# Input stage of a hybrid attention block: gate products of 256 tokens, smaller norm groups, x scaled on GpSimd

## The chip, the core and the metric

The kernel runs on one NeuronCore of a Trainium2 chip (trn2). The metric is the device time of one execution in microseconds (us), the median of several executions. Engine names as in the profile: PE is TensorE's matrix unit and PEld its weight loads, DVE is VectorE, ACT is ScalarE, POOL is GpSimd, SP is SyncE, whose queue starts the DMA transfers here (SPq).

## What is computed

One encoder block on x of 2048 tokens by 1024 channels, float32. x is RMS-normed, one input projection gives the queries, keys and values of two attention mixers, two gate paths and merge logits; the mixers' outputs are gated, projected, merged, projected again and added to x. Only its beginning matters here:

```python
h = rms_norm(x, norm_gain[layer])      # x * rsqrt(mean(x*x) + eps) * gain
proj = h @ w_in[layer]
qa, ka, va, qb, kb, vb, ga, gb, mg = jnp.split(proj, split_idx, axis=-1)
...
ya = ya.reshape(bsz, S, A_WIDTH) * jax.nn.silu(ga)
yb = yb.reshape(bsz, S, B_WIDTH) * jax.nn.silu(gb)
```

## The kernel before, in words

**Precision.** Every float32 factor is split into a float16 high part and a float16 low part, and a product is three float16 products: high by high, high by low, low by high. XH and XL hold the two parts of the normed x, turned so that channels lie on the partitions: 8 chunks of 128 channels by 2048 tokens. gh and gl are the parts of one block of 128 gate columns, wh and wl those of one "unit" (the projections of one attention group).

**Input stage.** x comes in 16 tiles of 128 tokens (x0 to x15), one 512 KB transfer each, with 14 buffers. A tile passes these steps:
- ACT squares it and sums along the row (`x_square`, L444);
- for a group of tiles, DVE turns the sums into mean plus epsilon (`x_stats`, L448) and takes a first guess of the inverse root (L256); three Newton rounds follow (`rs_newton`), on DVE for a group of two (L270 to L272, 9 small operations) and on POOL for a group of four (L265 to L268, 12 small operations). The groups before are x0-1, x2-3, x4-7, x8-11, x12-15;
- DVE multiplies the tile by its inverse root (`x_scale`, L458);
- PE transposes it, in two halves h0 and h1 of four 128x128 blocks each, into one of three PSUM buffers `s` (`x_turn`, L464);
- for each half ACT copies the high part to XH (`x_hi`, L467) and DVE subtracts to get XL (`x_lo`, L471). Only then the PSUM buffer is free.

Beside it the weights of gate columns c = 0, 1 and 2 are prepared: gain on POOL (`g_gain`, L320, two halves), squares on ACT (L328), a sum over partitions by a tiny matrix product (L189), a power-of-two scale by some seven small DVE operations (L196 to L204, L341), high part on ACT (L346), low part on DVE (L350). The weights of the first unit take the same way: gain on POOL (L175, four parts), squares on ACT (L214), high part on ACT (L231), low part on DVE (L237). `head_gain` (L479 to L488, twice) and two small scalings are more small DVE work.

**Gate products.** For each quarter q of 512 tokens and for c = 0 and 1 PE makes 24 products of 128x512 (8 chunks, three products each, L304) into one PSUM bank; then come a tanh on ACT (L367), a multiplication on DVE (L374) and a store from SP. A quarter needs four x tiles. "Warm" products on a constant (L498) fill PE before that. Behind the stage comes the first unit's projection, whose products are those of L647.

**What sets the order.** All instructions are put into a heap by a planned time (`at`), and the times come from tables at the top of the file (X_SQ, X_CH, X_G, X_W and so on). `stream` issues the 24 products of a block spread over 5.2 planned us, and between them whatever is due. The planned times fix only the order on each engine; every engine then works through its own instructions strictly in that order, and waits where an operand is missing.

Of the kernel before, what the change touches and what calls it, by code (L numbers as in the profile page):

```python
# [21 lines left out]
F32 = mybir.dt.float32  # L22
# [3 lines left out]
OP = mybir.AluOpType  # L26
# [6 lines left out]
NT = S // 128  # L33
NCH = D // 128
# [45 lines left out]
N_PREP = (6.3, 7.15, 7.5)  # L80
B_GAP = (0.25, 0.2, 0.22)
Y_MAX = (0.02, 0.8, 0.84)
X_SQ = (5.098, 1.401, 9.779, 2.051)
X_CH = (9.3, 2.65, 1.024, 0.955, 1.155, 1.305)
X_ST = (1.3, 0.179)
X_G = (7.5, 15.282, 45.87)
X_GP = (2.1, 5.694, 7.094, 7.694, 8.894, 10.194)
X_W = (14.0, 38.0, 48.0, 1.1, 4.8, 5.2, 6.3, 0.6, 50.255)
X_WARM = (24, 16, 16, 16, 12)
X_TH = (0.8, 2.173, 3.5)  # L90
# [17 lines left out]
def block_kernel(tc, x, w_units, w_gate, w_mrg, w_brn, w_out, w_bra, gain, qkg, sink, bias_a, bias_b, b_merge, out):  # L108
    nc = tc.nc
    V = nc.vector  # L110
    A = nc.scalar
    G = nc.gpsimd
# [7 lines left out]
    sm = es.enter_context(tc.tile_pool(name="sm", bufs=4))  # L120
# [10 lines left out]
    done = set()  # L131
# [127 lines left out]
    def rs_newton(a, yv, r, n, pool):  # L259

        t = sm.tile([128, 10], F32, name="rs_t")
        tv = t[:, :n]
        for i in range(3):
            if pool:
                G.tensor_tensor(tv, yv, yv, OP.mult)  # L265
                G.tensor_tensor(tv, tv, a, OP.mult)  # L266
# [3 lines left out]
            V.tensor_tensor(tv, yv, yv, OP.mult)  # L270
            V.scalar_tensor_tensor(tv, tv, -0.5, a, OP.mult, OP.mult)
            V.scalar_tensor_tensor(r if i == 2 else yv, tv, 1.5, yv, OP.add, OP.mult)  # L272
# [21 lines left out]
        for f in tproj_list(ps, wh, wl, c0, q, nch, XHt, XLt, ch0):  # L294
            f()

    def tproj_list(ps, wh, wl, c0, q, nch=NCH, XHt=XH, XLt=XL, ch0=0):
        n = 3 * nch
        ts = slice(512 * q, 512 * q + 512)
        out = []  # L300
        for ch in range(ch0, ch0 + nch):
            for w, xx in ((wh, XHt), (wh, XLt), (wl, XHt)):
                i = len(out)
                out.append(lambda w=w, xx=xx, ch=ch, i=i: T.matmul(  # L304
                    ps[:], lhsT=w[:, ch, c0:c0 + 128], rhs=xx[:, ch, ts], start=(i == 0), stop=(i == n - 1)))
        return out


    gw = {}
# [8 lines left out]
    def g_gain(c, i):  # L318
        v = gw[c][0][:, 4 * i:4 * i + 4, :]
        G.tensor_tensor(v, v, gn[:, 4 * i:4 * i + 4].unsqueeze(2).to_broadcast([128, 4, 128]), OP.mult)  # L320

    def g_square(c):
        pool = gp if c > 1 else sp0
# [62 lines left out]
    def at(t, f, *args):  # L386
        seq[0] += 1
        heapq.heappush(heap, (t, seq[0], f, args))
# [8 lines left out]
    def chain(steps):  # L397

        steps = sorted(steps, key=lambda e: e[0])
        done = [0]  # L400

        def go(k):
            if done[0] < k or steps[k][1](*steps[k][2:]) is False:
                at(now[0] + .04, go, k)
            else:
                done[0] = k + 1

        for k, e in enumerate(steps):
            at(e[0], go, k)
# [10 lines left out]
    xts, xss, xps = {}, {}, {}  # L420
# [12 lines left out]
        V.tensor_scalar(bmh[:], bmt[:], 0.5, None, OP.mult)  # L433


    groups = {0: (0, 1), 1: (0, 1), 2: (2, 3), 3: (2, 3)}
    groups.update((t, tuple(range(t - t % 4, t - t % 4 + 4))) for t in range(4, NT))

    def x_square(t):
        g = groups[t]  # L440
        if t == g[0]:
            xss[g] = [sm.tile([128, 4], F32, name="xss")]
        jk = sp0.tile([128, D], F16, name="jk")
        A.activation(jk[:], xts[t][:], AF.Square, accum_out=xss[g][0][:, t - g[0]:t - g[0] + 1])  # L444

# [4 lines left out]

    def x_newton(g):
        ss, y = xss[g]
        xss[g] = sm.tile([128, 4], F32, name="xr")
        rs_newton(ss, y, xss[g][:, :len(g)], len(g), len(g) > 2)

    def x_scale(t):
        i = t - groups[t][0]
        V.tensor_scalar(xts[t][:], xts[t][:], xss[groups[t]][:, i:i + 1], None, OP.mult)  # L458

    def x_turn(t, h):  # L460
        xps[t, h] = ps = s_p.tile([128, 4, 128], F32, name="s")
# [36 lines left out]
            T.matmul(ps[:, 0:256], lhsT=v[:, 0:128], rhs=v, start=True, stop=True)  # L498


    for t in range(XT_BUFS):
        at(.01 * t, x_load, t)
    at(.015, lambda: nc.sync.dma_start(out=gn[:], in_=gain))
    at(.035, g_load, 0)
    at(.075, g_load, 1)
    at(2.0, small_loads)

    def scale_time(t):
        return X_CH[0] + X_CH[1] * t

    def ready_time(t):
        return scale_time(t) + sum(X_CH[2:])

    for t, n in enumerate(X_WARM):
        at(scale_time(t) + X_CH[2] - .05 if t < 4 else scale_time(3) + X_CH[2] + X_CH[5] + .05, warm, n)
    for t in range(NT):
        b = X_SQ[0] + X_SQ[1] * t if t < 4 else X_SQ[2] + X_SQ[3] * (t - 4)
        at(b, x_square, t)
        if t == groups[t][-1]:
            at(b + X_ST[0], x_stats, groups[t])  # L520
            at(b + X_ST[0] + X_ST[1], x_newton, groups[t])
        b = scale_time(t)
        at(b, x_scale, t)
        for h in range(2):
            b = scale_time(t) + X_CH[2] + X_CH[5] * h
            at(b, x_turn, t, h)
            at(b + X_CH[3], x_hi, t, h)
            at(b + X_CH[3] + X_CH[4], x_lo, t, h)
        if t < 2:
            for k in range(2):  # L530
                at(ready_time(t) + 1.0 + 1.2 * k, x_again, t, (XH, XL)[k])
        if t + XT_BUFS < NT:
            at(ready_time(t), x_load, t + XT_BUFS)
    for c in range(3):
        b = X_G[c]
        if c == 2:
            at(X_G[0] + X_GP[5] + .1, g_load, c)
        chain([(b + X_GP[0] * i, g_gain, c, i) for i in range(2)]
              + [(b + d, f, c) for d, f in zip(X_GP[1:], (g_square, g_sum, g_pow, g_hi, g_lo))])
# [16 lines left out]
    pos = 0  # L556
    for q in range(4):
        ready = ready_time(4 * q + 3) + .1
        pos = max(pos, ready)
        until(pos)  # L560
        assert all(("x", t, h) in done for t in range(4 * q, 4 * q + 4) for h in range(2))
        for c in range(2):
            mm, after = g_step(c, q)
            pos = stream(pos, 5.2, mm)
            for k, f in enumerate(after):
                at(pos + X_TH[k], f)
    until(1e9)
    st.close()
# [492 lines left out]
    for u in range(NU + 1):  # L1061
        t = 8 * u
# [33 lines left out]
    t = 0  # L1096
# [472 lines left out]
```

## Time and profile before

| | us |
|---|---|
| median of three runs | 1982.05 (1981.57 to 1983.27) |
| profiled execution, its own time | 1981.84 |
| span of that execution, first to last instruction | 1980.0 |
| PE busy | 1949.6 (98%) |
| DVE, ACT, POOL busy | 1310.7 (66%), 1029.3 (52%), 944.1 (48%) |
| first product of the first unit starts (end of the input stage on PE) | 80.57 |

"Span" runs from the first to the last instruction, and the execution's own time lies 1.84 us above it. In a row of the timeline stand the start in us, the length in us, the engine, the line, the operation with output and input, the count, and in brackets the idle time of the engine before it and who ended that. Matrix products overlap in the records (a 128x512 product lasts 0.38 us and the next one starts 0.22 us later), so the distance between starts is what one costs. Rows that stand for several equal instructions run from the first start to the last end.

### The profile page before, as it was taken

To read this page: it belongs to the slowest core of one execution; us is meant where nothing else is said; L and a number is where in the kernel's file an instruction comes from. 1 tells how busy PE (TensorE), PEld (TensorE's weight loads), DVE (VectorE), ACT (ScalarE), POOL (GpSimd) and SP (SyncE) were. 2 spreads that over 40 slices of the span, in tenths; PEclk is the share of its full clock that TensorE was granted. 3 is DMA by queue.
4 is the path that set the end of the run, shared out by engine and by line. 5 is a ranking of instruction groups with operands and counts; after the bars stand their busy time and mean duration, and the time that the engine had idled before them with its cause. 6 is when DMAs were issued, how large, how long until landed. Compare 5 with 4: busy or idle time off the path is not lost.

```text
span 1980.0 us, 47987 instructions
## 1 busy us (share of the span) xinstructions
PE 1949.6 (98%) x17654; PEld 1396.6 (71%) x17654; DVE 1310.7 (66%) x3485; ACT 1029.3 (52%) x2369; POOL 944.1 (48%) x2430
## 2 busy tenths in 40 slices
PE   8999999999999999999999999999999999999999
PEld 5567896678878898888988879898544444444444
DVE  6679877888768876667776778767733232876412
ACT  7467656776555566555666655656433343432200
POOL 4254556455547755547666676666410100232533
PEclk8999999999999999999999999999999999999999
DMA  6248986897849696667767776756732334778763
GB/s 248 80 90 163 180 164 140 145 191 149 177 87 197 116 181 122 130 137 164 148 135 143 146 162 128 138 122 126 171 104 93 119 110 169 221 232 271 250 240 143
DMA packets 589501, 308.47 MB, mean 156 GB/s; under 512 B 458064, under 2 KB 526800, under 8 KB 587984
## 3 DMA queue, kind: packets, MB, share of 16 engines
q1 hardware_dynamic: 589264, 305.39, 66.3%
q8 instruction: 138, 2.26, 0.5%
q14 instruction: 99, 0.81, 0.1%
HBM read 129.91 MB, written 65.27 MB: 99 GB/s over the span
## 4 chain that ended last, share of the span: by engine, by line
PE 52%; DVE 4%; POOL 3%; issue 2%; DMA 2%; ACT 1%; SPq 0%; DVEq 0%; POOLq 0%; ACTq 0%
PE pj L647 19%; PE fps L304 17%; PE fps L1446 7%; PE pj L304 5%; PE s L801 2%; PE pv L850 2%; POOL rs_t L265 1%; DVE rw L711 1%; POOL rs_t L266 1%; DMA kq<-spl 1%; DVE qss L699 0%; POOL rs_t L267 0%; POOL rw L718 0%; DMA yg<-ytd 0%; DVE pr L816 0%
## 5 line engine op out<-in xcount | busy, mean ns | idle before, releaser
L647 PE MATMUL pj<-wh,XH 128*128 128x128 f16 (+2 forms) x2816 | 708.5, 268 | 6.9 <-DVE vt L687 6.8
L647 PE MATMUL pj<-wl,XH 128*128 128x128 f16 (+2 forms) x2816 | 714.8, 268 | 0.0
L647 PE MATMUL pj<-wh,XL 128*128 128x128 f16 (+2 forms) x2816 | 712.7, 269 | 0.0
L647 PEld LDWEIGHTS <-XH 128*128 128x128 f16 x5632 | 579.1, 113 | 71.3 <-issue 9.2
L647 PEld LDWEIGHTS <-XL 128*128 128x128 f16 x2816 | 316.4, 112 | 25.9
L816 DVE CUSTOM_DVE_ANT_0 pr<-s,b,ubuf 128x256 f32<-128x256 f32 (+3 forms) x512 | 218.8, 464 | 41.2 <-PE s L801 38.8
L304 PEld LDWEIGHTS <-wh 128*128 128x128 f16 x1280 | 124.8, 98 | 150.3 <-issue 2.7
L265 POOL TENSOR_TENSOR rs_t<-rs_y 128x8 f32<-128x8 f32 (+2 forms) x345 | 110.8, 321 | 180.2 <-DVE rs_y L256 123.6
L833 DVE SCALAR_TENSOR_TENSOR p<-pr,p 128x512 f16<-128x512 f32 (+2 forms) x256 | 185.5, 724 | 16.8 <-ACT p L829 16.2
L711 DVE TENSOR_TENSOR rw<-rw,qr 128x512 f32<-128x512 f32 (+1 forms) x112 | 119.2, 1064 | 101.8 <-POOL qr L268 87.8
L718 POOL TENSOR_TENSOR rw<-rw,g 128x128 f32<-128x128 f32 (+1 forms) x224 | 135.5, 624 | 84.3 <-DVE rw L711 58.6
L175 POOL TENSOR_TENSOR wraw<-wraw,gn 128x768 f32<-128x768 f32 (+1 forms) x80 | 108.3, 1360 | 130.1 <-DMA wraw<-in_w_mrg_dram 130.1
L829 ACT ACTIVATE p<-pr 128x512 f16<-128x512 f32 (+2 forms) x256 | 158.9, 621 | 11.6 <-DMA pt<-p 5.6
L304 PE MATMUL fps<-Y,wh 128*128 128x512 f16 x512 | 152.3, 379 | 0.3 <-DVE kp L1382 0.2
L801 PE MATMUL s<-kq 128*128 128x128 f16 (+1 forms) x1856 | 147.8, 218 | 4.7 <-DMA kq<-spl 4.5
L801 PEld LDWEIGHTS <-kq 128*128 128x128 f16 x2016 | 130.0, 98 | 28.8 <-issue 5.4
L666 ACT ACTIVATE rw<-pj 128x256 f32<-128x256 f32 (+1 forms) x224 | 86.1, 384 | 122.7 <-PE pj L647 119.2
L733 POOL COPY spl<-spl 128x256 f16<-128x256 f16 (+1 forms) x224 | 93.9, 448 | 116.9 <-DVE spl L728 115.2
L304 PE MATMUL pj<-XH,gh 128*128 128x512 f16 x384 | 145.5, 379 | 0.0
L304 PE MATMUL pj<-XL,gh 128*128 128x512 f16 x384 | 145.5, 379 | 0.0
L304 PE MATMUL pj<-XH,gl 128*128 128x512 f16 x384 | 145.5, 379 | 0.0
L1446 PE MATMUL fps<-wt,M 128*128 128x512 f16 x672 | 145.2, 379 | 0.0
(196 smaller groups left out, 3549.7 us busy)
## 6 DMA issues: line engine op xcount, KB each, us to landing
wraw<-in_w_units_dram SPq DMA_DIRECT2D x56, 384.0 KB, 4.6
mtd<-mm SPq DMA_DIRECT2D x56, 256.0 KB, 3.8
M<-mtd SPq DMA_DIRECT2D x8, 1792.0 KB, 9.7
mgd<-fg SPq DMA_DIRECT2D x40, 256.0 KB, 2.1
zd<-z SPq DMA_DIRECT2D x128, 66.0 KB, 1.9
zz<-zd SPq DMA_DIRECT2D x64, 132.0 KB, 3.0
xt<-in_x_dram SPq DMA_DIRECT2D x16, 512.0 KB, 8.9
gtd<-yo SPq DMA_DIRECT2D x32, 256.0 KB, 2.9
```

The costliest lines, as they stand in the source:

```text
L175: G.tensor_tensor(v, v, gn[:, c0:c0 + 2].unsqueeze(2).to_broadcast([128, 2, n]), OP.mult)
L265: G.tensor_tensor(tv, yv, yv, OP.mult)
L304: out.append(lambda w=w, xx=xx, ch=ch, i=i: T.matmul(ps[:], lhsT=w[:, ch, c0:c0 + 128], rhs=xx[:, ch, ts], start=(i == 0), stop=(i == n - 1)))
L647: out.append(lambda lhs=lhs, rhs=rhs, ch=ch, a=a, b=b, k=k: T.matmul(ps[:, a:b], lhsT=lhs[:, ch, :], rhs=rhs[:, ch, a:b], start=(k == 0), ...
L711: V.tensor_tensor(q, q, self.rr[:, :n].unsqueeze(2).to_broadcast([128, n, HD]), OP.mult)
L718: G.tensor_tensor(q[:, i, :un.nq, :], q[:, i, :un.nq, :], g, OP.mult)
L733: G.tensor_copy(sp[:, i, nh:, :, :], sp[:, i, nq:nh, ::-1, :])
L801: T.matmul(self.sv[j][:, o:o + k1 - k0], lhsT=q[:, h, :], rhs=kt[:, un.nq + kh + v * un.nk, k0:k1], start=(v == 0), stop=(v == 1))
L816: V.tensor_tensor_reduce(out=self.pv[:, j, self.p0:self.p0 + W], in0=self.sv[j], in1=un.bias[:, self.h0 + j, self.b0:self.b0 + W], scale=I ...
L829: A.activation(self.sp[:, :128 * n], self.pr, AF.Copy, scale=PSC)
L833: V.scalar_tensor_tensor(self.sp[:, 128 * n:], self.pr, PSC, self.sp[:, :128 * n], OP.mult, OP.subtract)
L1446: mm.append(lambda ch=ch, k=k, w=w, i=i: T.matmul(ps[:], lhsT=m[:, a, ch, k, :], rhs=wt[w][:, b, ch, :], start=(i == 0), stop=(i == 11)))
```

## The change

- A gate block is now 24 products of 128x256 for 256 tokens, so it needs two x tiles. The order is (c, h), with h the eighth of the tokens: (0,0), (0,1), (1,0), (1,1), and then c = 0, 1 for each h from 2 to 7. Two blocks share a PSUM bank, and tanh, multiplication and store follow the second. The banks alternate between two pools.
- x is normed in the groups x0-1, x2-3, x4-5, x6-9, x10-13, x14-15. All but the first do their Newton rounds on POOL.
- `x_scale` runs on DVE for x0 and x1 and on POOL for the other 14 tiles.
- The gain of c = 1 moves from POOL to DVE. The weights of c = 0 are loaded right behind x1 and gn, and those of c = 1 behind x5.
- 46 warm products are left of 84. The copies of the first two tiles behind the last one (`x_again`) come later.
- All planned times of the stage are new.

```diff
-X_WARM = (24, 16, 16, 16, 12)
+X_SC = (9.2, 9.9, 15.8, 17.475, 23.6, 24.8, 33.0)
+X_WARM = (34, 6, 6, 0)
...
-    def tproj_list(ps, wh, wl, c0, q, nch=NCH, XHt=XH, XLt=XL, ch0=0):
+    def tproj_list(ps, wh, wl, c0, q, nch=NCH, XHt=XH, XLt=XL, ch0=0, n=512):
+        ts = slice(n * q, n * q + n)
...
-    groups = {0: (0, 1), 1: (0, 1), 2: (2, 3), 3: (2, 3)}
-    groups.update((t, tuple(range(t - t % 4, t - t % 4 + 4))) for t in range(4, NT))
+    groups = {t: g for g in ((0, 1), (2, 3), (4, 5), (6, 7, 8, 9), (10, 11, 12, 13), (14, 15)) for t in g}
...
-        rs_newton(ss, y, xss[g][:, :len(g)], len(g), len(g) > 2)
+        rs_newton(ss, y, xss[g][:, :len(g)], len(g), g[0] > 0)
...
-        V.tensor_scalar(xts[t][:], xts[t][:], xss[groups[t]][:, i:i + 1], None, OP.mult)
+        (V if t < 2 else G).tensor_scalar(xts[t][:], xts[t][:], xss[groups[t]][:, i:i + 1], None, OP.mult)
...
-    for q in range(4):
-        ready = ready_time(4 * q + 3) + .1
-        pos = max(pos, ready)
+    for c, h in [(0, 0), (0, 1), (1, 0), (1, 1)] + [(c, h) for h in range(2, 8) for c in range(2)]:
+        pos = max(pos, ready_time(2 * h + 1) + .1, (X_G0, X_G1)[c][5] + .1)
         until(pos)
...
+        if h % 2 == 0:
+            banks[c] = (pv_p if q % 2 else pj_p).tile([128, 512], F32, name="pv" if q % 2 else "pj")
+        ps = banks[c]
+        o = 256 * (h % 2)
+        pos = stream(pos, 2.6, tproj_list(ps[:, o:o + 256], gh, gl, 0, h, n=256))
+        if h % 2:
+            for k, f in enumerate(gate_steps(ps, c, q, ih, None)):
                 at(pos + X_TH[k], f)
```

**Place 1, tiles x6 and x7.** On PE before, from x4 on, the transposes of a half tile (L464, four of them) are set apart from the next ones by gate products (L304): by three between the halves of x4, shown here, and by six after that, x6 and x7 included:

```order
L464 MATMUL s<-idf,xt 128x128 x4
L304 LDWEIGHTS gh
L304 MATMUL pj<-XH,gh 128x512
L304 LDWEIGHTS gh
L304 MATMUL pj<-XL,gh 128x512
L304 LDWEIGHTS gl
L304 MATMUL pj<-XH,gl 128x512
L464 MATMUL s<-idf,xt 128x128 x4
```

Now all 16 transposes of x6 and x7 (both halves of both tiles, L467) stand together behind the 144th gate product, the last of block (1,2), and right behind them comes block (0,3), which reads x6 and x7:

```order
L308 LDWEIGHTS gl
L308 MATMUL pv<-XH,gl 128x256
L467 MATMUL s<-idf,xt 128x128 x16
L308 LDWEIGHTS gh
L308 MATMUL pv<-XH,gh 128x256
```

No gate product stands any more between these transposes and the first product that needs their result. On POOL, now, the last of the 12 Newton operations for x6-9 (output `xr`) is followed by the scaling of x6, the fourth part of the first unit's gain (`wraw`), and the scaling of x7 and x8:

```order
L272 TENSOR_TENSOR xr<-rs_t,rs_y 128x4
L461 TENSOR_SCALAR xt<-xt,xr 128x1024
L179 TENSOR_TENSOR wraw<-wraw,gn 128x768
L461 TENSOR_SCALAR xt<-xt,xr 128x1024 x2
L324 TENSOR_TENSOR graw<-graw,gn 128x512 x2
L461 TENSOR_SCALAR xt<-xt,xr 128x1024
```

Before, POOL scaled no x tile, and all four parts of the unit's gain came behind the last Newton round.

**Place 2, tiles x7 to x9 on ACT.** Before, the copies to XH (L467) of the later tiles come in runs of four with a tanh (L367) between, since all squares of x are done by then:

```order
L367 ACTIVATE yo<-pj,ubuf 128x512
L467 ACTIVATE XH<-s 128x4x128 x4
L367 ACTIVATE yo<-pj,ubuf 128x512
L467 ACTIVATE XH<-s 128x4x128 x4
L367 ACTIVATE yo<-pj,ubuf 128x512
L467 ACTIVATE XH<-s 128x4x128 x3
```

Now there stand, from the two copies of x7 on (first row): the squares of x13, a copy of x8, squares of the unit's weights (`wsq`), a copy of x8, the squares of x14 and of gate column 2, weights again, a copy of x9, a tanh, a copy of x9:

```order
L470 ACTIVATE XH<-s 128x4x128 x2
L447 ACTIVATE jk,xss<-xt 128x1024
L470 ACTIVATE XH<-s 128x4x128
L218 ACTIVATE wl,wsq<-wraw 128x768
L470 ACTIVATE XH<-s 128x4x128
L447 ACTIVATE jk,xss<-xt 128x1024
L332 ACTIVATE gh,gsq<-graw 128x1024
L218 ACTIVATE wl,wsq<-wraw 128x768
L470 ACTIVATE XH<-s 128x4x128
L371 ACTIVATE yo<-pv,ubuf 128x512
L470 ACTIVATE XH<-s 128x4x128
```

So weight and square work has moved between the copies. In the same way the squares of x9 now stand behind the copies of x5.

**Place 3, the last tiles on DVE.** Now, behind the second `head_gain` (its last two operations are the first rows), the low parts of the unit's weights (`wl`) and the multiplications for the gates (`yo`) stand between the subtractions (`XL`) of x14 and x15:

```order
L490 TENSOR_SCALAR ubuf<-ubuf 128x1
L491 TENSOR_SCALAR ubuf<-ubuf 128x1
L241 SCALAR_TENSOR_TENSOR wl<-wraw,ubuf,wh 128x768
L474 TENSOR_TENSOR XL<-s,XH 128x4x128
L436 TENSOR_SCALAR nsnk<-snk 128x8
L437 TENSOR_SCALAR bmh<-bmt 128x16
L378 SCALAR_TENSOR_TENSOR yo<-yo,pj 128x512
L241 SCALAR_TENSOR_TENSOR wl<-wraw,ubuf,wh 128x768
L474 TENSOR_TENSOR XL<-s,XH 128x4x128 x2
L378 SCALAR_TENSOR_TENSOR yo<-yo,pj 128x512
L474 TENSOR_TENSOR XL<-s,XH 128x4x128
```

Before, the last subtraction of the stage (first row) is followed by the scale of gate column 2, and only then by the first `wl` (L237):

```order
L471 TENSOR_TENSOR XL<-s,XH 128x4x128
L196 TENSOR_REDUCE wm_913<-pt 128x1
L197 TENSOR_SCALAR wm_913<-wm_913 128x1
L199 TENSOR_SCALAR pw_p<-wm_913 128x1
L200 TENSOR_SCALAR pw_p<-pw_p 128x1
L203 TENSOR_SCALAR ubuf<-pw_p 128x1
L204 RECIPROCAL ubuf<-ubuf 128x1
L341 TENSOR_SCALAR ubuf<-ubuf 128x1
L237 SCALAR_TENSOR_TENSOR wl<-wraw,ubuf,wh 128x768
```

What moved is the order of DVE alone: all four `wl`, and with them the low part of gate column 2, now come ahead of the last subtraction.

More of the change, by code (lines that the diff above doesn't have):

```diff
@@ L441, in x_square @@
         if t == g[0]:
-            xss[g] = [sm.tile([128, 4], F32, name="xss")]
+            xss[g] = [sm.tile([128, 5], F32, name="xss")]
         jk = sp0.tile([128, D], F16, name="jk")
@@ L498, in warm @@
             T.matmul(ps[:, 0:256], lhsT=v[:, 0:128], rhs=v, start=True, stop=True)
+    at(0, warm, X_WARM[0])
     for t in range(XT_BUFS):
@@ L554, in stream @@
         return pos + share
-    pos = 0
-    for q in range(4):
-        ready = ready_time(4 * q + 3) + .1
-        pos = max(pos, ready)
+    pos, banks = 0, {}
+    for c, h in [(0, 0), (0, 1), (1, 0), (1, 1)] + [(c, h) for h in range(2, 8) for c in range(2)]:
+        pos = max(pos, ready_time(2 * h + 1) + .1, (X_G0, X_G1)[c][5] + .1)
         until(pos)
[L561 to L565, printed above, removed]
+        assert ("g", c) in done and all(("x", t, k) in done for t in (2 * h, 2 * h + 1) for k in range(2))
+        gh, gl, ih = gw[c][:3]
+        q = h // 2
+        if h % 2 == 0:
[5 more added lines that the diff above has]
+            for k, f in enumerate(gate_steps(ps, c, q, ih, None)):
                 at(pos + X_TH[k], f)
```

47 lines of the change are left out of this document (24 added, 23 removed).

## The prediction

> **What bounds the kernel now.** I read the page's busy times first, then busy times by stretch, then the timeline.
>
> ```profile
> PE 1949.6 (98%) x17654; PEld 1396.6 (71%) x17654; DVE 1310.7 (66%) x3485; ACT 1029.3 (52%) x2369; POOL 944.1 (48%) x2430
> ```
>
> ```profile
> 0.00:28.04 28.04, 19.20 (x118) 14.54 (x118) 16.49 (x45) 19.45 (x34) 12.62 (x26) 0.82 0.94 357
> 28.04:80.57 52.53, 52.50 (x294) 30.56 (x295) 41.81 (x96) 34.49 (x59) 15.41 (x33) 1.00 0.17 67
> 80.57:130.00 49.43, 49.12 (x334) 29.27 (x333) 27.00 (x61) 21.70 (x48) 23.76 (x71) 1.00 0.37 101
> ```
>
> A stretch's row has its length, then the busy time of PE, PEld, DVE, ACT and POOL, the granted clock, the DMA share and GB/s. PE bounds the kernel: it has no gap from 28.04 to 80.57, where the first unit starts, and hardly one behind that (49.12 of 49.43 us). So whatever moves the end of the input stage moves the end of the kernel by as much. The change can only gain in the first 28 us, in which PE warms up or waits for x.
>
> PE's work, by the distance between starts:
>
> ```profile
> 28.54 0.38 PE L304 MATMUL pj<-XH,gh 128*128 128x512 f16 x1
> 28.75 0.38 PE L304 MATMUL pj<-XL,gh 128*128 128x512 f16 x1
> ...
> 50.11 0.60 PE L464 MATMUL s<-idf,xt 128*128 128x128 f32 x4
> 50.55 0.38 PE L304 MATMUL pj<-XH,gh 128*128 128x512 f16 x1
> ```
>
> ```profile
> 700.34 0.27 PE L647 MATMUL pj<-wh,XH 128*128 128x256 f16 x1
> ...
> 701.87 0.27 PE L647 MATMUL pj<-wh,XL 128*128 128x256 f16 x1
> ```
>
> A 512-wide product costs 0.215 us, four transposes 0.44. The two 256-wide products are 14 steps apart, 0.109 each, every one with its own weight load. So the halved products cost nothing much: 384 x 0.109 = 41.9 against 192 x 0.215 = 41.3. What counts is when PE starts and where it stops again.
>
> **The first product.** Tiles arrive one after another:
>
> ```profile
> 8.57 1.06 ACT L444 ACTIVATE jk<-xt 128x1024 f16<-128x1024 f32 x1 [1.70 <-DMA xt<-in_x_dram]
> ...
> 12.81 1.06 ACT L444 ACTIVATE jk<-xt 128x1024 f16<-128x1024 f32 x1 [1.84 <-DMA xt<-in_x_dram]
> ```
>
> Here ACT waited for x2 and for x4. x2 is the third 512 KB, x4 the sixth (gate column 0 lies between): 4.24 / 3 = 1.4 us each. Now column 0 comes third, so x2 arrives at 10.0 and x3 at 11.4. The groups up to 80.6 us, with the mean in ns behind the comma:
>
> ```profile
> L467 ACT ACTIVATE XH<-s 128x512 f16<-128x512 f32 x32 | 18.8, 593 | 13.8 <-PE s L464 13.5
> L444 ACT ACTIVATE jk<-xt 128x1024 f16<-128x1024 f32 x16 | 16.8, 1053 | 6.2 <-DMA xt<-in_x_dram 6.1
> L367 ACT ACTIVATE yo<-pj,ubuf 128x512 f32<-128x512 f32 x7 | 4.8, 684 | 1.1 <-PE pj L304 0.9
> L214 ACT ACTIVATE wl<-wraw 128x768 f16<-128x768 f32 x4 | 3.3, 836 | 0.0
> L328 ACT ACTIVATE gh<-graw 128x1024 f16<-128x1024 f32 x3 | 3.1, 1048 | 0.0
> L444 ACT ACTIVATION_READ_ACCUMULATOR jk<-xt 128x1 f32 x16 | 3.1, 192 | 0.0
> ```
>
> ```profile
> L471 DVE TENSOR_TENSOR XL<-s,XH 128x512 f16<-128x512 f32 x32 | 21.6, 687 | 8.2 <-ACT XH L467 8.1
> L374 DVE SCALAR_TENSOR_TENSOR yo<-yo,pj 128x512 f32<-128x512 f32 x7 | 4.8, 682 | 0.1
> L237 DVE SCALAR_TENSOR_TENSOR wl<-wraw,ubuf,wh 128x768 f16<-128x768 f32 x4 | 4.0, 1014 | 0.2 <-ACT wh L231 0.2
> L350 DVE SCALAR_TENSOR_TENSOR gl<-graw,ubuf,gh 128x1024 f16<-128x1024 f32 x3 | 3.8, 1278 | 0.0
> ```
>
> ```profile
> L175 POOL TENSOR_TENSOR wraw<-wraw,gn 128x768 f32<-128x768 f32 x4 | 6.6, 1688 | 0.0
> L320 POOL TENSOR_TENSOR graw<-graw,gn 128x512 f32<-128x512 f32 x6 | 6.3, 1062 | 9.8 <-DMA graw<-in_w_gate_dram 9.8
> L475 POOL COPY XH<-XH 128x1024 f16<-128x1024 f16 x2 | 2.1, 1034 | 3.1 <-ACT XH L467 3.1
> masks.py:199 POOL TENSOR_SCALAR_AFFINE_SELECT idf<-idf 128x128 f32<-128x128 f32 x1 | 0.3, 292 | 0.1
> ```
>
> From 10.0 ACT squares x2, column 0 and x3 in a row, 1.25 each (with 0.19 for the sum): 13.75. On PE the norm product of column 0 now stands ahead of the second half of x0, which waits for that square. Then the first XH (0.59), its XL (0.69), and, queued behind it on DVE, mean and guess of x2-3 (0.4): 15.45. Their Newton rounds move to POOL:
>
> ```profile
> 7.31 0.16 DVE L270 TENSOR_TENSOR rs_t<-rs_y 128x2 f32<-128x2 f32 x1
> ...
> 9.07 0.75 DVE L458 TENSOR_SCALAR xt<-xt,xr 128x1024 f32<-128x1024 f32 x1
> ...
> 22.26 1.28 DVE L350 SCALAR_TENSOR_TENSOR gl<-graw,ubuf,gh 128x1024 f16<-128x1024 f32 x1
> ...
> 22.48 1.12 POOL L266 TENSOR_TENSOR rs_t<-rs_t,xss 128x4 f32<-128x4 f32 x1
> ...
> 43.77 0.20 POOL L265 TENSOR_TENSOR rs_t<-rs_y 128x4 f32<-128x4 f32 x1 [5.61 <-DVE rs_y L256]
> ...
> 44.88 0.20 POOL L265 TENSOR_TENSOR rs_t<-rs_y 128x4 f32<-128x4 f32 x1
> ```
>
> Nine operations on DVE took 9.07 - 7.31 = 1.76; on POOL four take 1.11, so twelve 3.3. The pair in the middle shows a lock: a 0.20 us operation of POOL lasts 1.12 and ends with DVE's `gl`. The column-1 gains that move to DVE have no row there: between the XL row (0.69) and POOL's own (1.06); I take 0.69, and DVE has slack at that point. With one collision (0.7) POOL's rounds end at 19.4.
>
> **Scaling on POOL** has no row. The low end is DVE's own 0.75 (the 9.07 row), the high end twice POOL's 1.06 for 512 elements, 2.1. But those 512 are read from two tensors, and the scaling reads one; the one-input rows, 1024 in 1.03 and 128 float32 in 0.29, give about 0.8 ns an element for either type. I take 1.03. Of the Trainium skill, GPSIMD Engine Reference, section 8, calls DVE about twice as fast for elementwise work; that estimate, 2 x 0.75, would add some 1.4 us over the three scalings of the chain below. Its section 4.1 puts one-input operations near line rate, and the copy row agrees with that.
>
> So x2 is scaled at 20.4, turned at 21.4 (0.94 on a slow clock), and the first gate product starts there, 7 us earlier than before.
>
> **Block (0,0)** has 24 products, three half tiles and a norm product ahead of block (0,1): 2.6 + 1.3 + 0.3 = 4.2 at full clock. But PE has been idle for some 3 us before it, and then
>
> ```profile
> 24.20 0.94 PE L464 MATMUL s<-idf,xt 128*128 128x128 f32 x4 [1.08 <-DVE XL L471]
> ```
>
> ```profile
> 25.00:26.00 1.00, 1.00 (x6) 0.50 1.05 393
> 28.00:29.00 1.00, 0.93 (x7) 1.00 1.04 406
> ```
>
> the granted clock (behind the count) stays at half from 24.2 to 28: 3.8 us that do 1.9 of work. Block (0,1) starts at 21.4 + 4.2 + 1.9 = 27.5 (26.5 if tiles land earlier or the clock holds, 28.2 if column 1's seven small DVE operations delay the last XL).
>
> **Tiles x6 and x7.** From 27.5 PE has 120 products and four half tiles: 13.1 + 1.8, and would be through at 42.4. x9's square stands behind the copies of x5, whose last transposes come 53 products and four half tiles into this: 35.1. XH 0.6, square 1.25, mean and guess 0.4: 37.3. POOL: Newton 3.3, x6 1.03, a gain 1.69, x7 1.03: 44.4. Then transposes 0.44, two XH 1.18, XL 0.69: block (0,3) starts at **46.7**. Of the wait 1.8 us is transposing and **2.5 idle**.
>
> **ACT from x7 to x9.** Behind the last XH of x7 (46.0) come two squares of x (2.49), column 2's (1.24), two of the unit's weights (2.06), four XH (2.37) and a tanh (0.68): 8.84, then XL 0.69. Block (0,4) starts at **55.5**. PE's own work (48 products 5.25, four half tiles 1.75, a norm product 0.3) ends at 54.0: **1.5 idle**.
>
> **DVE to x15.** From 55.5 to the last XL its queue holds 12 XL (8.25), 4 `yo` (2.75), 4 `wl` (4.05), `gl` (1.28), two scales of 7 and 6 small operations at 1.76 / 9 = 0.196 (2.55), mean, guess and two small ones (0.75), and two `head_gain`:
>
> ```profile
> 64.10 0.22 DVE L479 SCALAR_TENSOR_TENSOR g<-qg 128x64 f32<-128x64 f32 x1
> ...
> 65.66 0.68 DVE L374 SCALAR_TENSOR_TENSOR yo<-yo,pj 128x512 f32<-128x512 f32 x1
> ```
>
> 1.56 each. Together 22.75. `gl` and `wl` then meet POOL's scalings of x13 to x15 in the lock: nothing if they miss each other, 2 us if each waits; I take 1. The last XL ends at **79.3**. PE alone (144 products 15.7, twelve half tiles 5.3, a norm product) would be there at 76.8: **2.5 idle**.
>
> **Sum.** The last two blocks take 5.25: 84.5 in place of 80.57, **+4.0 us**: the early start is given back in three waits. The profiled execution took 1981.84; with +4.0 that is 1985.9, and against the median 1982.05 1986.1. The removed warm products are waited for by nobody, and the later copies on POOL are read only by later units.
>
> **Rivals.** A difference under 0.2%, 4 us, cannot be told from none; my forecast lies on that border.
> - *The three waits as worked out*, 0.45: bounds of first block (-1.0, +0.7), lock (-1, +1) and gains give 1983.7 to 1988.5. 0.28 of it is slower.
> - *Part of the waits is absorbed*, since one that ends earlier shortens the next: first block at 26.5, no lock, x9's square up to a microsecond sooner: 0 to +2, 1982 to 1984. 0.16, same.
> - *The early start is kept*: if x7 is turned before PE is through with the 144th product, at 42.4, so POOL done with it 4.3 us sooner than worked out, and ACT and DVE keep ahead after that. PE's work behind 21.4 is 41.9 + 27 x 0.44 + 0.9 = 54.7: the end is 76.1, or 78.0 with the slow clock, 1976.5 to 1979.5. For it speaks that before PE ran 52 us without a gap with DVE at 80%; against it the orders, which leave no product between x7's transposes and their user. 0.16; 0.10 of it faster.
> - *Scaling costs 2.1*: x2, x6 and x7 lie on the chain, +3.2 more: 1989.3. Against it the copy row. 0.11, slower.
> - *The clock falls again in the waits*: a stall at half clock costs up to 1.9 us as above; behind x7 1.5 of it is hidden by ACT's queue, before the last blocks nothing: +2.3 more, 1988.4. 0.12, slower. The Trainium skill's TensorE: Matmul & The Clock Gate (Part 1) lets the clock fall only after an idle window of about 3.4 us; by that these waits would leave it alone, but the 24.20 row shows a fall after a wait of 1.08 in a thinly filled stretch.
>
> Faster 0.10, same 0.17 + 0.16 + 0.06 = 0.39, slower 0.51. The range runs from the rival that keeps the start to the dearer scaling, 1979.0 to 1990.0.
>
> **What would show it.** In the new profile: the first gate product near 21.4 at half clock; scaling on POOL near 1.03; PE idle for DVE's XL around 43 to 47, around 54, and before the last two blocks; the first unit at 84.5. It is wrong if PE has no gap behind block (0,0), if `gl` or the 256-wide products are what waits, or if the first unit starts at the old time and later work pays.

## The result, and the profile after

The changed kernel takes 1995.45 us in the median of four runs (1994.67 to 1998.08), and the kernel before, beside it, 1982.66. The ratio is 1.006, with a 95% interval from 1.0045 to 1.0074: slower, and above the upper end of my range, 1990.0. The profiled execution took 1995.38 us, 13.54 more than that of before.

The line of the page that answers to the first one shown of before, and two stretches of the input stage, in the same columns as before (length; busy time of PE, PEld, DVE, ACT and POOL; granted clock; DMA share; GB/s):

```profile
PE 1948.1 (98%) x17808; PEld 1413.3 (71%) x17808; DVE 1302.4 (65%) x3466; ACT 1029.4 (52%) x2369; POOL 980.6 (49%) x2466
```

```profile
28.00:40.00 12.00, 12.00 (x111) 10.87 (x110) 7.29 (x12) 9.84 (x18) 11.14 (x12) 1.00 0.41 159
40.00:95.00 55.00, 43.31 (x361) 37.43 (x360) 28.83 (x70) 28.97 (x52) 42.56 (x53) 0.94 0.06 25
```

The page's busy line hides the loss: PE is at 98% as before, and POOL at 49% after 48%. The stretch shows it. Before, PE had no gap from 28.04 to 80.57; now it is idle for 11.7 of the 55 us behind 40, DVE and ACT are only half busy, and POOL is the busiest of the three helpers. Whom PE waits for in the first 100 us (us in total, times, longest):

```profile
PE s L467 <- POOL xt L461: 17.2, 7, 5.9
PE s L467 <- DVE xt L461: 4.6, 1, 4.6
PE pv L501 <- DVE ones L142: 1.1, 1, 1.1
PE pv L308 <- DVE XL L474: 0.3, 1, 0.3
```

Seven waits are for a tile scaled by POOL. The waits that I had worked out for ACT's queue and for DVE's last subtractions are not there: ACT itself waits for PE's transposes (26.6 us in all between 20 and 95). On POOL, at the place of x6 to x8:

```profile
42.53 2.84 POOL L461 TENSOR_SCALAR xt<-xt,xr 128x1024 f32<-128x1024 f32 x1
45.34 1.47 POOL L179 TENSOR_TENSOR wraw<-wraw,gn 128x768 f32<-128x768 f32 x1
46.80 5.66 POOL L461 TENSOR_SCALAR xt<-xt,xr 128x1024 f32<-128x1024 f32 x2
```

One scaling takes **2.84 us**, where I took 1.03 and put the upper bound at 2.1. On PE the first, the second and the third wait, and the first product of the unit:

```profile
22.80 1.12 PE L467 MATMUL s<-idf,xt 128*128 128x128 f32 x4 [5.87 <-POOL xt L461]
...
45.43 1.09 PE L467 MATMUL s<-idf,xt 128*128 128x128 f32 x8 [1.31 <-POOL xt L461]
49.69 1.62 PE L467 MATMUL s<-idf,xt 128*128 128x128 f32 x8 [3.17 <-POOL xt L461]
...
95.19 0.33 PE L655 MATMUL pj<-wh,XH 128*128 128x384 f16 x1
```

The first unit starts at 95.19 in place of 80.57, **+14.6 us**, and 13.5 of it stand at the end. That is the theory tested below: the price of POOL's scaling made the loss, and POOL became the bound of the stage. The rivals: the order, with x6 and x7 turned in one bunch, costs the time whoever scales; or POOL's other new work (Newton rounds) does.

### The profile page after: what moved, and what is told of

The parts are those of the page before. It is cut to its first block, busy times and chain, and to the rows that moved or that the text cites. A ratio compares the mean times of both kernels' runs of the same rounds, so it can differ in the third digit from the quotient of the medians.

```text
span 1993.5 us, 48316 instructions
## 1 busy us (share of the span) xinstructions
PE 1948.1 (98%) x17808; PEld 1413.3 (71%) x17808; DVE 1302.4 (65%) x3466; ACT 1029.4 (52%) x2369; POOL 980.6 (49%) x2466
## 4 chain that ended last, share of the span: by engine, by line
PE 75%; POOL 9%; DVE 7%; issue 5%; DMA 3%; ACT 1%; SPq 1%; DVEq 0%; POOLq 0%; ACTq 0%
PE pj L655 30%; PE fps L308 19%; PE pj L308 11%; PE fps L1454 7%; PE s L809 4%; PE pv L858 3%; POOL rs_t L269 1%; POOL xt L461 1%; POOL rs_t L270 1%; DVE rw L719 1%; POOL rs_t L271 1%; DVE qss L707 1%; DVE pr L824 1%; DMA xt<-in_x_dram 1%; POOL rw L726 1%
## 5 line engine op out<-in xcount | busy, mean ns | idle before, releaser
L269 POOL TENSOR_TENSOR rs_t<-rs_y 128x8 f32<-128x8 f32 (+3 forms) x351 | 110.6, 315 | 172.8 <-DVE rs_y L260 122.3
L1397 POOL TENSOR_TENSOR kp<-kp,fg 128x512 f32<-128x512 f32 x32 | 44.5, 1392 | 209.8 <-DVE fg L1390 121.0
L308 PE MATMUL pj<-XH,gh 128*128 128x512 f16 (+1 forms) x384 | 139.4, 363 | 0.0
L732 ACT ACTIVATE spl<-rw 128x512 f16<-128x512 f32 (+1 forms) x112 | 72.1, 643 | 130.4 <-POOL vt L682 84.8
```

The costliest lines, as they stand in the source:

```text
L308: out.append(lambda w=w, xx=xx, ch=ch, i=i: T.matmul(ps[:], lhsT=w[:, ch, c0:c0 + 128], rhs=xx[:, ch, ts], start=(i == 0), stop=(i == n - 1)))
```

## The experiments

In all of them "the first unit" is the start of the first product of that kind in the profiled execution, 80.57 before and 95.19 after. The execution's own time less that start lies between 1899.0 and 1903.8 us in all kernels of the study that were profiled for their time, so the start tells what the stage costs to about 2 us, in that execution. The profiled execution lies between 2.6 us below and 4.4 us above the median of its kernel, so a start and a ratio need not agree to better than that. Ratios are to runs of the kernel before on the same chip.

### All scaling on DVE

```
-        (V if t < 2 else G).tensor_scalar(xts[t][:], ...
+        V.tensor_scalar(xts[t][:], ...
```

> The change with one part of it undone: all sixteen tiles are scaled on DVE. The price theory (a scaling takes 2.84 us on POOL, and nothing else of the change costs more than I worked out): no wait for POOL's xt is left on PE, and the first unit product starts between 81 and 85 us instead of 95.2, so that the run takes 1982 to 1987 us. The order theory (the bunched transposes and their queues cost the time whoever scales): PE still waits over 10 us between 28 and 80 us, the first unit product starts at 90 or later, 1990 us or more. What is left over 1982 is the price of all the rest of the change; my prediction worked out +4.0 for it.

Measured: the first unit at 82.00, ratio 0.999 (0.9981 to 0.9998), 13.2 us of the 14.6 gone. PE still waits for scaled tiles, now DVE's:

```profile
PE s L467 <- DVE xt L461: 10.7, 6, 4.9
```

4.9 of this is the wait for x0 and 3.1 that for x2, ahead of the first gate product, which leaves 2.7 for four others. The rest of the change, all but the engine of the scaling, is worth +1.4 us on the stage, where I had worked out +4.0.

### The kernel before, with its scaling on POOL

```
-        V.tensor_scalar(xts[t][:], ...
+        (V if t < 2 else G).tensor_scalar(xts[t][:], ...
```

> The kernel before with that part alone: tiles x2 to x15 are scaled on POOL. The price theory: 2.84 us each, four in a row for a group of four, 11.4 us where DVE took 3.0; POOL also has the Newton rounds and gains, and PE eats a group of four in 13.8 us, so that POOL becomes the bound: the first unit product moves from 80.6 to between 89 and 95 us, 1990 to 1997 us. The rival, that the groups and the order of the changed kernel are needed to make a loss: scaling stays hidden behind the 52 us without a gap, 1981 to 1985 us.

Measured: the first unit at 94.93, ratio 1.0073 (1.006 to 1.0087). One line put into the kernel before makes the whole loss. The tile's view (shortest, median and longest in ns) and a stretch of the stage:

```profile
L458 POOL TENSOR_SCALAR xt<-xt,xr x14: 2840/2845/3197, 14.4 to 77.1; 128x1024 f32<-128x1024 f32 x14
```

```profile
60.00:70.00 10.00, 8.84 (x51) 4.90 (x49) 4.58 (x8) 3.84 (x7) 10.00 (x6) 1.00 0.07 26
```

POOL (the last busy time) has no idle time left in this stretch, DVE and ACT are idle more than half of it: POOL is the bound. Groups, halved products and the new times are not needed for the loss.

### Another form: the product of two tensors

```
-            G.tensor_scalar(xts[t][:], xts[t][:], r, None, OP.mult)
+            G.tensor_tensor(xts[t][:], xts[t][:], r.to_broadcast([128, D]), OP.mult)
```

> The change with POOL's scaling written as a product of two tensors, the second one the tile's one column of scales repeated along the row. If POOL's price is one of the form (a product with a scalar taken from a column), this costs what POOL's gains cost, 1.9 to 2.1 ns an element: 2.0 us instead of 2.84, the first unit product near 87 us, 1986 to 1989 us. If POOL takes 2.8 ns for any product of 1024 float32 of one tile, nothing changes: 95 us, 1995 us.

Measured: 1.89 us a scaling, as expected, but the first unit at 90.07, 3 us later than I had said, ratio 1.0033 (1.0021 to 1.0045). The form sets the price. What I had left out shows on DVE, in the groups between 20 and 96 us (busy, mean ns | idle), first of this run and then of the changed kernel:

```profile
L354 DVE SCALAR_TENSOR_TENSOR gl<-graw,ubuf,gh 128x1024 f16<-128x1024 f32 x2 | 4.8, 2402 | 0.3 <-ACT gh L350 0.3
L451 DVE TENSOR_SCALAR xss<-xss 128x2 f32<-128x2 f32 (+1 forms) x4 | 4.7, 1176 | 0.7 <-ACT jk L447 0.7
```

```profile
L354 DVE SCALAR_TENSOR_TENSOR gl<-graw,ubuf,gh 128x1024 f16<-128x1024 f32 x3 | 4.0, 1326 | 0.3 <-ACT gh L350 0.3
L451 DVE TENSOR_SCALAR xss<-xss 128x2 f32<-128x2 f32 (+1 forms) x4 | 1.8, 458 | 0.8 <-ACT jk L447 0.8
```

The cheaper form holds DVE up more: a mean of two or four numbers, 0.16 us alone in the kernel before, lasts 1.18 on average, and in the 70 us from 20 to 90 DVE is busy for 48.90 us, where the changed kernel has 38.97 up to its first unit. The Newton rounds do not start later for it: at 23.75, 53.34 and 63.38 they begin 0.1 us behind POOL's own work ahead of them. PE waits 1.2 us for XL and 0.6 for `gl`, more than in the changed kernel; what makes up the 3 us was not separated.

### A constant in place of the column of scales

```
-            G.tensor_scalar(xts[t][:], xts[t][:], r, None, OP.mult)
+            G.tensor_scalar(xts[t][:], xts[t][:], SX, None, OP.mult)
```

> The change with POOL's scaling by a constant, 1024, in place of the tile's own column of scales; it leaves the norm of x2 to x15 out. If the column is what costs, the scaling takes about the 1.03 us that I predicted, PE waits for it little, and the first unit product is at 81 to 86 us, 1982 to 1988 us: then this run is also the test of my prediction's sum, +4.0 us. If the operation itself costs 2.84 us on POOL whatever the scalar is, the run is that of the change: 95 us, 1995 us.

Measured: 2.77 us a scaling, the first unit at 96.16, ratio 1.0063 (1.0049 to 1.0077). The column of scales is not what costs (in this kernel x2 to x15 are not normed); this left open why one tensor and one factor are dearer than two tensors.

### The same instruction on 368 columns

```
+        n = D if t < 2 else 368
-        ...tensor_scalar(xts[t][:], xts[t][:], ...
+        ...tensor_scalar(xts[t][:, :n], xts[t][:, :n], ...
```

> The change with POOL scaling only the first 368 of the 1024 columns of x2 to x15; it leaves the norm of the other columns out. At 2.84 us for 1024 columns a scaling then costs about 1.02 us, the price that my prediction took, so that the run tests the rest of my sum. The price theory: the first unit product starts at 84.5 us, as I worked out (82 to 85.5), 1983 to 1987 us. The rival, that POOL's other work (Newton rounds, gains, copies) or its queue sets the stage at any price: 88 us or later, 1989 us or more. If the price hardly falls with the columns, 95 us.

Measured: 1.20 us a scaling, the first unit at 82.34, ratio 0.9984 (0.9975 to 0.9993). With the price near mine the stage ends 2.2 us before my sum, and the loss is gone.

### POOL's prices by themselves

> The kernel before with a row of eleven further POOL operations on scratch tiles put at its very start, where DVE has hardly any work; its time means nothing. It measures the disputed price by itself. By columns: a product with a column of scales takes 2.84 us for 1024 float32, 1.42 for 512 and 0.71 for 256 if it goes by the element; near 2.8 for all if it is a fixed cost. By type: if bytes set it, float16 in and out takes about half, 1.4; if elements do, 2.8. By form: a float32 copy of 1024 takes 1.03 like the float16 copy if what I took for the scaling held for copies at least, and about 2 if only the type made that row cheap; the product of two tensors takes 1.9.

Measured, in the timeline of POOL at the start of that kernel (start, length; p is float32, h float16, s the column of scales). The rows at 14.76 and 17.31 are the ones that surprised:

```profile
3.07 2.85 POOL L446 TENSOR_SCALAR bp<-bp,bs 128x1024 f32<-128x1024 f32 x1
6.02 1.56 POOL L447 TENSOR_SCALAR bp<-bp,bs 128x512 f32<-128x512 f32 x1
7.68 0.92 POOL L448 TENSOR_SCALAR bp<-bp,bs 128x256 f32<-128x256 f32 x1
8.69 2.85 POOL L449 TENSOR_SCALAR bh<-bp,bs 128x1024 f16<-128x1024 f32 x1
11.63 3.16 POOL L450 TENSOR_SCALAR bh<-bh,bs 128x1024 f16<-128x1024 f16 x1
14.76 1.05 POOL L451 TENSOR_SCALAR bp<-bp 128x1024 f32<-128x1024 f32 x1
...
17.31 1.04 POOL L453 CAST bh<-bp 128x1024 f16<-128x1024 f32 x1
...
20.73 1.89 POOL L455 TENSOR_TENSOR bp<-bp,bs 128x1024 f32<-128x1024 f32 x1
```

The price goes by the element: (2.85 - 0.92) / 768 = 2.5 ns each and about 0.3 fixed. An effect of the type does not show: float32 to float16 takes the same 2.85, and the row with 3.16, float16 on both sides, began while a scaling of DVE (10.64 to 12.08) was still running. A float32 copy took 1.37, beside another scaling of DVE. But the row at 14.76, "times 1.0, plus 0.0", is the same instruction with a second operation, and takes 1.05.

### Multiply and add in one instruction

```
-            G.tensor_scalar(xts[t][:], xts[t][:], r, None, OP.mult)
+            G.tensor_scalar(xts[t][:], xts[t][:], r, 0.0, OP.mult, OP.add)
```

> The change with one thing different: POOL multiplies by the column of scales and adds 0.0 in the same instruction, as the Newton rounds' own multiply-and-add does. In the run of POOL's prices the one instruction with two operations (times 1.0, plus 0.0) took 1.05 us for 1024 float32, where every product with a column and no second operation took 2.85. Theory A, the second operation is what makes it fast: the scaling takes about 1.05 us, just the price of my prediction; the first unit product starts at 81.5 to 84.5 us, 1980 to 1986 us. Theory B, the column of scales is slow (the fast one had constants): about 2.85 us, 95 us, 1995 us.

Measured: 1.13 us a scaling, the first unit at 81.88, ratio 0.9992 (0.9983 to 1.0). Every instruction stands in the same place as in the changed kernel; only the scaling's form differs. POOL at the place shown above, and the stretch from 20 us to the first unit, of this run and of the changed kernel:

```profile
40.87 1.13 POOL L465 TENSOR_SCALAR xt<-xt,xr 128x1024 f32<-128x1024 f32 x1
41.96 1.47 POOL L179 TENSOR_TENSOR wraw<-wraw,gn 128x768 f32<-128x768 f32 x1
43.41 2.22 POOL L465 TENSOR_SCALAR xt<-xt,xr 128x1024 f32<-128x1024 f32 x2
```

```profile
20.00:82.00 62.00, 57.62 (x503) 51.31 (x504) 38.92 (x91) 41.01 (x73) 39.40 (x76) 0.97 0.28 106
```

```profile
20.00:95.00 75.00, 60.51 (x501) 52.88 (x502) 38.97 (x92) 41.75 (x75) 60.98 (x75) 0.91 0.22 85
```

DVE's and ACT's work is the same to 2%. POOL's falls by 21.6 us, and the stage by 13.3. The price theory is shown: the loss of the change is in one operand left at "none", and neither the order nor POOL's Newton rounds, which are the same in both, make it.

### Which forms are fast

> The kernel before with nine further POOL operations on scratch tiles at its very start; its time means nothing. 128x1024 float32 in place unless said: column times and plus 0.0; constant times alone; constant times and plus; constant times and times; column times and times 1.0; constant plus alone; constant times and plus on 512 columns; the same on float16; column times and plus, float32 to float16. Theory A (the form with a second operation is fast): 1.05 wherever there are two operations, 2.8 for times alone and plus alone. Theory A2 (only multiply-then-add is fast): also 2.8 for times and times. Theory B (a column is slow): 2.85 for the three with a column.

Measured, rows in the order of that list:

```profile
3.06 1.12 POOL L445 TENSOR_SCALAR bp<-bp,bs 128x1024 f32<-128x1024 f32 x1
4.27 2.78 POOL L446 TENSOR_SCALAR bp<-bp 128x1024 f32<-128x1024 f32 x1
7.14 1.05 POOL L447 TENSOR_SCALAR bp<-bp 128x1024 f32<-128x1024 f32 x1
8.27 1.05 POOL L448 TENSOR_SCALAR bp<-bp 128x1024 f32<-128x1024 f32 x1
9.42 1.12 POOL L449 TENSOR_SCALAR bp<-bp,bs 128x1024 f32<-128x1024 f32 x1
10.62 3.12 POOL L450 TENSOR_SCALAR bp<-bp 128x1024 f32<-128x1024 f32 x1
...
15.55 1.12 POOL L453 TENSOR_SCALAR bh<-bp,bs 128x1024 f16<-128x1024 f32 x1
```

Theory A: 1.05 to 1.12 wherever there are two operations, multiply-and-multiply too, and 2.78 to 3.12 with one (beside the 3.12 DVE scaled a tile from 12.10 to 12.85). The column adds 0.07, and float16 takes 1.04, so the type again shows no effect.

### The order written anew, on DVE

```
-X_SQ = (..., 21.678, 2.449)
-X_SC = (..., 33.0)
+X_SQ = (..., 17.6, 2.4)
+X_SC = (..., 27.9)
-    groups = ... (4, 5), (6, 7, 8, 9), (10, 11, 12, 13), (14, 15)
+    groups = ... (4, 5), (6, 7), (8, 9, 10, 11), (12, 13, 14, 15)
```

with all sixteen tiles scaled on DVE, as in the first experiment, a pitch X_CH[1] of 2.6 for 2.493, the unit's gains (X_W[1]) at 33.0 for 27.434 and the head gains (X_W[8]) at 60.0 for 52.691.

> All scaling on DVE, as in the run with the first unit product at 82.0 us, and the order written anew: groups of norms (6,7), (8 to 11), (12 to 15), their squares earlier, x6 to x15 scaled 2.6 us apart in the order's own times and from 27.9 instead of 33.0, the head gains behind the stage. If what gives the early start back is the order (x6 and x7 turned in one bunch behind the 144th product, DVE busy with head gains before x14), PE has under 1.5 us of waits behind 28 us and the first unit product starts at 77 to 79.5, 1977 to 1980 us, faster than both. If it is DVE's or ACT's own load, it stays at 81 to 83, 1982 to 1984 us.

Measured: the first unit at 79.54, ratio 0.9977 (0.9969 to 0.9986): faster than before and than the change, just beyond the edge of what I had expected, with one wait of 2.51 where I had said under 1.5 in all. Who made it, on PE and on DVE:

```profile
46.19 0.27 PE L308 MATMUL pv<-XL,gh 128*128 128x256 f16 x1 [2.51 <-DVE XL L474]
```

```profile
43.60 1.93 DVE L461 TENSOR_SCALAR xt<-xt,xr 128x1024 f32<-128x1024 f32 x1 [2.83 <-POOL xr L272]
45.46 1.27 DVE L474 TENSOR_TENSOR XL<-s,XH 128x512 f16<-128x512 f32 x2
```

PE waits for the XL of x7, whose operands had been there since 41.6; in DVE's queue the scaling of x8 stands ahead of it and waits for POOL's norm of x8 to x11. The scaling itself then lasts 1.93 in place of 0.75, beside a gain that POOL starts at 43.52, so that 1.2 of the 2.51 come from the two engines holding each other up.

### ... with the Newton rounds of x2 and x3 on DVE

```
-        rs_newton(ss, y, ..., len(g), g[0] > 0)
+        rs_newton(ss, y, ..., len(g), g[0] > 2)
```

> The run before this one with one edit more: the Newton rounds of x2 and x3 are taken by DVE (1.8 us there, 3.3 to 3.7 on POOL). If the chain through x2 sets the first gate product, it starts some 1.5 us sooner and the first unit product by up to as much, 0.5 to 1.5 us; if the column 0 of gate weights is what comes last there, no difference.

A miss: the first gate product came at 21.99 in place of 20.42, the first unit at 81.17, ratio 0.9989 (0.998 to 0.9997). On POOL the rounds ran beside DVE's last XL of x1; on DVE they stand behind it, from 17.97 on, so x2 was scaled at 20.22 instead of 19.06. In this run PE's clock also rose later, at 16.3 in place of 14.7, and the traces tell most of the 1.6 us apart: that last XL starts 0.8 later (17.36 in place of 16.57), behind work of PE at half clock, and the transposes of x2 take 0.88 in place of 0.46 up to the first gate product. About 1.2 us are thus the clock, and the remaining 0.4 the edit: by this reckoning the same clock would not have brought a gain either.

### ... with norms in pairs

```
-    groups = ... (6, 7), (8, 9, 10, 11), (12, 13, 14, 15)
+    groups = ... (6, 7), (8, 9), (10, 11), (12, 13), (14, 15)
```

> The respread order with all scaling on DVE, and norms in pairs of tiles from x8 on instead of fours. In that order's run PE waited once behind the first products, 2.51 us at 43.7 for the XL of x7, which stood in DVE's queue behind the scaling of x8, which waited for the Newton rounds of its four. With pairs x9's square is the last one needed, 5 us sooner. If that chain is the wait, it goes, and the first unit product starts near 77 us instead of 79.5, 1977 to 1979 us. If POOL's extra Newton rounds (two more of 3.3 us) or DVE's load (94 to 96% between 60 and 80 us) take its place, 79 to 81 us.

Measured: the first unit at 76.83, 1974.41 us (1977.62 in the profiled execution), ratio **0.9954** (0.994 to 0.9967), the best kernel of the study. The wait of 2.51 is gone; PE from 40 us on:

```profile
40.00:51.00 11.00, 11.00 (x103) 10.15 (x102) 9.30 (x16) 8.02 (x16) 9.51 (x23) 1.00 0.07 25
51.00:60.00 9.00, 8.72 (x82) 7.92 (x80) 6.26 (x16) 6.89 (x15) 7.85 (x20) 1.00 0.15 58
60.00:70.00 10.00, 10.00 (x94) 9.26 (x93) 9.62 (x18) 7.86 (x12) 4.25 (x4) 1.00 0.07 28
```

This is the end that my rival of the kept early start gave, 76.1 to 78.0.

### ... and the scaling on POOL in its fast form

> The pair order of the run before this one, but with x2 to x15 scaled on POOL as times-and-plus-0.0 (1.12 us each there, 0.75 on DVE). It separates the engine from the order. If the order alone kept the early start, the first unit product stays at 76.8 to 78.5 us and the run at 1974 to 1978 us, with DVE relieved of 10.5 us of work. If POOL cannot carry it at any price, since in the pair order it is busy 9.5 of 11 us between 40 and 51 us without the scalings, PE waits for POOL's xt there by some 3 to 5 us again and the first unit product starts at 80 to 82.5 us, 1979 to 1984 us: then the order helps only where the engine that scales has room.

A miss beyond both: the first unit at 88.73, ratio 1.0014 (1.0005 to 1.0023), though a scaling takes 1.12. The profiled execution, 1991.38, is the slowest of eleven (median 1986.98), so that a usual start may be some us earlier. POOL's queue tells most of it:

```profile
25.37 0.20 POOL L272 TENSOR_TENSOR xr<-rs_t,rs_y 128x2 f32<-128x2 f32 x1
29.18 0.19 POOL L269 TENSOR_TENSOR rs_t<-rs_y 128x2 f32<-128x2 f32 x1 [3.61 <-ACT gh L350]
...
33.24 3.31 POOL L465 TENSOR_SCALAR xt<-xt,xr 128x1024 f32<-128x1024 f32 x3
...
45.74 0.20 POOL L269 TENSOR_TENSOR rs_t<-rs_y 128x2 f32<-128x2 f32 x1 [4.54 <-DVE rs_y L260]
```

```profile
28.93 0.17 DVE L260 TENSOR_SCALAR rs_y<-xss 128x2 int32<-128x2 int32 x1
```

The scales of x4 were ready at 25.6. But the Newton rounds of x6 and x7 stand ahead of its scaling. They wait 3.61 us, until DVE has made their first guess at 29.1 (the second fence; the bracket names ACT, which ended in the same moment), and then run for 4, so x4 is scaled at 33.24. The same happens to x8: its scales are ready at 40.1, but the rounds of x10 and x11 stand ahead and wait 4.54 (the last row of the first fence), and it is scaled at 50.38. Block (1,0) starts 1.3 us later than in the pair order, block (1,1) behind x4 5.9 and block (1,3) behind x8 10.0, the first unit 11.9. In an order made for scaling on DVE, what POOL waits for stands in front of what it could do. Neither the engine nor the order decides alone: what counts is what stands ahead in the queue of the engine that scales.

## Why the prediction was wrong, step by step

The failed step is **"Scaling on POOL has no row ... I take 1.03"**. It measured 2.84, above the bound of 2.1 too. The row that I chose, a copy of 1024, is a fast form; the two-input gain that gave the upper bound is a middle one; a single product with a column is the slowest of the three. The 14 scalings of 2.84 made POOL the bound of the stage, where I had POOL on the chain at three tiles only. With the price at 1.13, in the kernel that differs in nothing else, each step stands beside what I worked out (start on PE in us):

| step | predicted | with 1.13 | the change, 2.84 |
|---|---|---|---|
| first gate product | 21.4 | 21.93 | 23.71 |
| block (0,1) | 27.5 | 27.56 | 29.01 |
| through 144 products | 42.4 | 42.44 | 43.95 |
| block (0,3) | 46.7 | 45.93 | 51.14 |
| block (0,4) | 55.5 | 53.67 | 60.81 |
| block (0,7) | 79.3 | 76.64 | 89.95 |
| first unit | 84.5 | 81.88 | 95.19 |

- **The halved products** cost 0.109 as said, **the Newton rounds** on POOL 3.3 where DVE left them alone (x4 and x5: 22.36 to 25.63). The first product came 0.5 late and the slow first block took 0.5 less than I gave it; from block (0,1) to the 144th product the sum is right to 0.1 us.
- **Tiles x6 and x7**: the bunch was there, and POOL was done with x7 at 44.5 (I had 44.4). The block started 0.8 earlier than said. I let it wait for the last XL; its products of the tiles' second halves come only after 12 x 0.109 = 1.3 us of others.
- **ACT from x7 to x9 and DVE to x15**: 1.1 us more and then 0.8. It is the same mistake, since with 1.13 the last XL of x9 ends at 54.59 and that of x15 at 77.65, each about 1 us behind the start of the block that reads it. And I added up lengths, while the records of one engine overlap by some 0.1 us: ACT's work from the last XH of x7 (46.37) to the last of x9 (53.86) took 7.49, not 8.84. Of the 1.5 and 2.5 us idle nothing came; with 1.13 PE waits there 0.36, 0.69 and 0.17 for POOL's tiles. The lock term was real: two `wl` and one `gl` there lasted 0.78, 0.77 and 0.20 us over their rows of before, 1.75 where I took 1.
- **+4.0** for the stage was therefore 2.6 too much; measured +1.3 with 1.13 and +1.4 on DVE. At the price that I had assumed the change is worth nothing (ratio 0.9992), so that it is slower, as just over half of my chances said, is luck: the waits that I forecast did not make it so.
- **The rival "the early start is kept"** has a slip: an end at 76.1 in place of 80.57 gives 1977.4 to 1977.6, not 1976.5, and the range from 1979.0 leaves most of this rival out.
- **The rival "scaling costs 2.1"** had the mechanism, with too low a price and a wrong count. It charged x2, x6 and x7. The 1.71 us between the two prices came to 13.3 on the stage, nearly eight tiles: once POOL is the bound, every scaling between two waits lies on the chain, not only those of the tiles for which PE waits in the cheap case.
- **"The clock falls again in the waits"** held too, as a consequence. Granted clock (third from the end) in two stretches behind the wait of 3.17 for x7:

```profile
50.00:51.00 1.00, 1.00 (x8) 1.00 (x7) 0.00 (x0) 0.51 (x1) 1.00 (x1) 0.55 0.00 0
51.00:52.00 1.00, 0.66 (x4) 0.26 (x3) 0.72 (x2) 0.74 (x3) 1.00 (x1) 0.50 0.00 0
```

The clock stays at half for 3.4 us there (50.1 to 53.5) and once more behind the wait of 3.31 (63.8 to 67.2), and in the run with 1.13 not at all behind 28 us. So behind 28 us at most half of these 6.8 us, 3.4 of the 13.3, can be the clock; how much of it is was not separated.

## What to carry to other kernels

Before work is moved to another engine, take its price there from a row of the same operation in the same form, or measure it with a few instructions on scratch data at the kernel's start; one run does it, and here it would have shown a factor of 2.5 hanging on one operand. A row of another form bounds nothing, and the engine's whole queue of such operations has to be added up against the stage, not only those on the chain. An order tuned for one engine's prices does not carry over: look at what stands ahead of each moved instruction, and at what that waits for.

## What the runs showed of the hardware

- **A TENSOR_SCALAR with one operation takes POOL 2.5 to 2.7 times as long as one with two.** 128x1024: 2.77 to 2.85 us for "times" alone with a constant or a column, 1.05 to 1.13 for "times, then plus or times"; two tensors 1.89; a cast 1.04. Why the second operation makes it fast, no run shows. The Trainium skill's GPSIMD Engine Reference, section 4.1, calls one-input operations roughly line-rate; that fits the forms with two operations and the cast, and the form that this kernel used takes 2.84 / 1.04 = 2.7 times as long as the cast.
- **Each form holds DVE up, the slow one for part of its time only.** In the first run of POOL's prices a DVE operation of 0.16 us that starts beside the scaling of 8.69 lasts 1.04; the next four take 0.16 each (the second row is the first of them), while the scaling runs on to 11.54:

```profile
8.78 1.04 DVE L271 SCALAR_TENSOR_TENSOR rs_t<-rs_t,xss 128x2 f32<-128x2 f32 x1
9.85 0.16 DVE L272 SCALAR_TENSOR_TENSOR rs_y<-rs_t,rs_y 128x2 f32<-128x2 f32 x1
```

In the changed kernel, too, a `g` of 0.22 us, begun 0.2 behind the start of a scaling, lasts 0.95 (82.44), and a `gl` begun 1.3 behind one takes its usual 1.28 (30.22); near a scaling's end operations are held again (a `g` of 0.26 lasts 0.75, 84.44). Beside the two-operation form a `wl` lasts 1.78 (65.96) in place of 1.01, and beside the two-tensor form a 0.16 us mean lasts 1.89. In sum the fast form costs DVE no more than the slow one: from 20 us to the first unit it is busy for 38.92 us with the one and 38.97 with the other; the two-tensor form costs it 10 us more.

- **PE's clock falls after waits shorter than 3.4 us, and not by their length alone.** In the last run it dropped to 0.5 within 2 us of a wait of 2.15 us (49.4 to 51.55); in the order written anew it stayed at full through one of 2.51 (43.68 to 46.19). First the last run, then the other:

```profile
51.00:52.00 1.00, 0.45 (x4) 0.45 (x5) 0.00 (x0) 0.00 (x0) 1.00 (x2) 1.00 0.00 0
52.00:53.00 1.00, 1.00 (x9) 0.83 (x8) 0.13 (x1) 0.60 (x1) 1.00 (x2) 0.71 0.00 0
53.00:54.00 1.00, 1.00 (x6) 0.90 (x5) 1.00 (x2) 0.00 (x0) 1.00 (x2) 0.50 0.00 0
```

```profile
46.00:47.00 1.00, 0.81 (x8) 0.77 (x8) 1.00 (x3) 0.00 (x0) 1.00 (x2) 1.00 0.00 0
```

Each stay at half in the runs of this study lasts 3.4 us or two or three times that, in the last run from 52.4 to 55.8, in the other from 21.6 to 25.0. Counted on from there in steps of 3.41 us, the wait of 2.15 lies whole in one step (49.0 to 52.4), and the wait of 2.51 is cut in two at 45.45 (1.77 and 0.74). That fits a clock that is set anew at fixed steps by how busy PE was in the step. But no one idle time parts all cases (a step with 1.75 idle, 21.0 to 24.4 in the kernel before, was followed by a fall), and no run was made to test it. The Trainium skill's TensorE: Matmul & The Clock Gate (Part 1) gives an idle window of about 3.4 us that runs freely; the free running fits the difference between the two, a full idle window does not fit the first.
